# Placing a feed-forward part's ordinary units by a running count of VectorE work over TensorE work

## The chip, the cores and the metric

The kernel runs on one core of a Trainium2 chip. TensorE (PE in the profile) does the matmuls, VectorE (DVE) and ScalarE (ACT) the work on elements, GpSimd (POOL) a few small operations and some DMA issues, SyncE (SP) most DMA issues. Each engine takes its instructions in the order of the built program. The metric is the device time of one execution in microseconds; lower is better.

## The reference

Two decoder layers on 256 tokens of width 2048, all in float32:

```python
for l in range(DEPTH):                      # DEPTH = 2
    h = rms_norm(x, norm1_g[l])
    z = h @ w_in[l]                         # 2048 x 3584
    z_sgu = jax.nn.gelu(z[..., :2 * SGU_WIDTH], approximate=False)
    out_a = chunked_sgu(z_sgu, sgu_norm_g[l], sgu_w[l], sgu_b[l])
    out_b = swa_sink_attention(...)
    mixed = jnp.concatenate([rms_norm(out_a, out_norm_a[l]), rms_norm(out_b, out_norm_b[l])], axis=-1)
    x = x + mixed @ w_out[l]                # 2048 x 2048
    h2 = rms_norm(x, norm2_g[l])
    x = x + (jax.nn.silu(h2 @ w_gate[l]) * (h2 @ w_up[l])) @ w_down[l]   # 2048 x 5632, twice, and 5632 x 2048
```

The last line is the feed-forward part, and the only part that the change touches.

## The kernel before, in words

**Exact products.** PE multiplies in a reduced float32 form (`F32R`), so each operand is split into a high and a low part, and each product takes three matmuls (`mm3`, L126): high x high, high x low, low x high. The weights are split on the fly: a *unit* loads 256 x 512 weights into one of seven `raw` buffers (L88, queue of SP), ACT copies them into `wh` (L97), DVE subtracts into `wl` (L98); `wh` and `wl` have four buffers each.

**Two kinds of unit.** In the feed-forward part the 5632 columns are 11 blocks of 512. Blocks 3 to 10 are computed for gate and up together in a form like Strassen's, with seven products of half size in place of eight (`seven`, L571); I call their units *own units*. An own unit has 6 matmuls (`s_unit`, L574). A block has a *first half* (L588 to L607): four rounds of four own units, into four banks `m0` to `m3`. Three additions of weights on DVE stand before three of the four units of a round (L595, L598, L601), and one accumulating load by POOL (L603). At the *turn* the four banks are combined (L608 to L616). The *second half* (L619 to L628) has four rounds of three own units into banks `n0` to `n2`, without additions. Then the block is closed (L629 to L635), and its activations are transposed later (`act_later`, L567, due 2 and 3 ticks on; an ordinary unit is one tick, an own unit half of one).

Blocks 0 to 2, and all of the product with `w_down`, are *ordinary units* with 12 matmuls each (`unit`, L131), into one pair of banks `dacc` while the own units run. `gate_up` (L654) gives 16 units to a block; `down` (L668) gives units for one or two blocks at a time, for four column blocks in turn, and evacuates after each (L683). Before it may start, the activations of its blocks must have been transposed; until then it gives no unit, but says False (L670, L671): a *refusal*. `STD_ORDER` sets the order: gate and up of block 0, down of 0 and 3, gate and up of 1, down of 1 and 4, of 5 and 6, gate and up of 2, down of 2 and 7, of 8 and 9, of 10.

**How the two are mixed.** `s_stream` yields after every own unit and says by how much the ordinary stream, `other`, is owed (L696 to L703): 0.575 of a unit in a first half, 0.23 in a second half. When a whole unit is owed, one is emitted; at the turn and at the end of a block two are emitted whatever is owed. What is refused stays owed. When all own units are out, the rest of `other` runs alone (L705). A scheduler then orders each engine's instructions, with emission as priority, so that the built order follows the emitted one with small shifts.

Of the kernel before, what the change touches and what calls it, by code (L numbers as in the profile page):

```python
# [24 lines left out]
NTOK = SEQ // P  # L25
# [19 lines left out]
    ("gu", 0), ("down", (0, 3)), ("gu", 1), ("down", (1, 4)), ("down", (5, 6)), ("gu", 2),  # L45
    ("down", (2, 7)), ("down", (8, 9)), ("down", (10,)),
)
SHARE_A = 0.575
SHARE_B = 0.23
TURN = 2  # L50
RL = 512
WARM = 12

# [12 lines left out]
def trunk(ctx, tc, x, xt, w_in, w_out, w_gate, w_up, w_down, sgu_w, sgu_g, consts,  # L66
# [14 lines left out]
    def f(t):  # L81
        return t.bitcast(F32)
# [8 lines left out]
    def split2(raw):  # L91
        wh = wp.tile([P, 2, NB], F32R, tag="wh", name="wh", bufs=4)
        wl = wp.tile([P, 2, NB], F32R, tag="wl", name="wl", bufs=4)
        step = 2 if clock[0] > 1 else 1
        for j in range(0, 2, step):
            src = raw[:, j : j + step, :]
            nc.scalar.copy(wh[:, j : j + step, :], src)  # L97
            nc.vector.tensor_tensor(  # L98
                wl[:, j : j + step, :], src, f(wh[:, j : j + step, :]), ALU.subtract
            )  # L100
        return wh, wl

    clock = [0]
    serial = itertools.count()
    pending = []

# [24 lines left out]
    def unit(src, acts, acc, first, last):  # L131
        raw = raw_load(src, 2 if clock[0] < 4 else 1)
        wh, wl = split2(raw)
        for j in range(2):
            act, aj = acts[j]
            for t in range(NTOK):
                ts = slice(t * P, (t + 1) * P)
                mm3(
                    acc[t], act[:, 0, aj, ts], act[:, 1, aj, ts], wh[:, j, :], wl[:, j, :],
                    first and j == 0, last and j == 1,  # L140
                )
        tick()

    def product(srcs, pairs):
# [114 lines left out]
    for lay in range(L):  # L259
# [299 lines left out]
        def act_T(b, c, sg, pairs_f=pairs_f):  # L559
            ps = pm.tile([P, 2, SEQ], F32, tag="sm", name="ps_f")  # L560
            transpose_pair([sg[t][:, 2 * c * P : (2 * c + 2) * P] for t in range(NTOK)], ps)
            pair = tp.tile([P, 2, 2, SEQ], F32R, tag="aT", name="aT")
            nc.scalar.copy(pair[:, 0], ps)
            nc.vector.tensor_tensor(pair[:, 1], ps, f(pair[:, 0]), ALU.subtract)
            pairs_f.setdefault(b, []).append(pair)

        def act_later(b, sg, act_T=act_T):  # L567
            for c in range(2):
                later(2 + c, lambda c=c: act_T(b, c, sg))

        def seven(b, lay=lay, pairs2=pairs2, ext2=ext2, act_later=act_later):  # L571
            bank = [pa.tile([P, NB], F32, tag="acc", name=f"m{i}") for i in range(4)]

            def s_unit(raw, m, i, op, first, last):  # L574
                wh, wl = split2(raw)
                for j in range(2):
                    ah, al = (op(2 * i + j, h) for h in range(2))
                    mm3(bank[m], ah, al, wh[:, j, :], wl[:, j, :], first and j == 0, last and j == 1)
                tick(0.5)

            def a_op(k, t):
                return lambda p, h: pairs2[p][:, h, k, t * P : (t + 1) * P]

            def e_op(n):
                return lambda p, h: ext2[p][:, h, n, :]

            kept = []
            for i in range(4):  # L588
                b11 = raw_load(w_gate[lay, b, i, 0])
                b12 = raw_load(w_up[lay, b, i, 0])  # L590
                b22 = raw_load(w_up[lay, b, i, 1])
                t1 = wp.tile([P, 2, NB], F32, tag="raw", name="t1", bufs=7)
                t2 = ap.tile([P, 2, NB], F32, tag="spt", name="t2", bufs=4)
                first, last = i == 0, i == 3
                nc.vector.tensor_tensor(t1, b11, b12, ALU.add)  # L595
                s_unit(b11, 0, i, a_op(0, 0), first, last)
                yield SHARE_A
                nc.vector.tensor_tensor(t2, t1, b22, ALU.add)  # L598
                s_unit(t1, 1, i, e_op(1), first, last)
                yield SHARE_A  # L600
                nc.vector.tensor_tensor(b12, b12, b22, ALU.add)  # L601
                s_unit(t2, 3, i, e_op(2), first, last)
                nc.gpsimd.dma_start(t2, w_gate[lay, b, i, 1], accum_op=ALU.add)  # L603
                yield SHARE_A
                s_unit(b12, 2, i, e_op(0), first, last)
                yield SHARE_A
                kept.append(t2)  # L607
            m1 = zp.tile([P, NB], F32, tag="z", name="m1")  # L608
            nc.scalar.copy(m1, bank[0])
            u1 = zp.tile([P, NB], F32, tag="z", name="u1")  # L610
            nc.vector.tensor_tensor(u1, bank[3], m1, ALU.add)
            c22 = zp.tile([P, NB], F32, tag="z", name="c22")
            c21 = zp.tile([P, NB], F32, tag="z", name="c21")
            nc.vector.tensor_tensor(c21, bank[2], u1, ALU.add)
            nc.vector.tensor_tensor(c22, bank[1], c21, ALU.add)
            nc.vector.tensor_tensor(u1, bank[1], u1, ALU.add)  # L616
            yield "turn"
            bank = [pa.tile([P, NB], F32, tag="acc", name=f"n{i}") for i in range(3)]
            for i in range(4):  # L619
                b21 = raw_load(w_gate[lay, b, i, 1])  # L620
                b22 = raw_load(w_up[lay, b, i, 1])
                first, last = i == 0, i == 3
                s_unit(b21, 0, i, a_op(1, 0), first, last)
                yield SHARE_B
                s_unit(kept[i], 1, i, a_op(1, 1), first, last)
                yield SHARE_B
                s_unit(b22, 2, i, e_op(3), first, last)
                yield SHARE_B  # L628
            sg = [m1, c21]  # L629
            for t, m in ((0, m1), (1, c21)):  # L630
                nc.vector.tensor_tensor(m, bank[t], m, ALU.add)
                nc.scalar.activation(m, m, AF.Silu, scale=rstd2[t])
            nc.vector.tensor_tensor(u1, bank[2], u1, ALU.add)
            for t, c in ((0, u1), (1, c22)):
                nc.vector.scalar_tensor_tensor(sg[t], c, nrstd2[t], sg[t], ALU.mult, ALU.mult)  # L635
            act_later(b, sg)
            yield "turn"

        seven_done = [False]

# [13 lines left out]
        def gate_up(b, even=even, act_later=act_later):  # L654
            acc = yield from even(b, w_gate)
            sg = []
            for t in range(NTOK):
                s = zp.tile([P, NB], F32, tag="z", name="sg")
                nc.scalar.activation(s, acc[t], AF.Silu, scale=rstd2[t])
                sg.append(s)  # L660
            acc = yield from even(b, w_up)
            for t in range(NTOK):
                nc.vector.scalar_tensor_tensor(
                    sg[t], acc[t], rstd2[t], sg[t], ALU.mult, ALU.mult
                )
            act_later(b, sg)

        def down(blocks, final, lay=lay, pairs_f=pairs_f, norm_block=norm_block, ss1=ss1, pairs1=pairs1):  # L668
            for n in range(ND):
                while any(len(pairs_f.get(b, [])) < 2 for b in blocks):  # L670
                    yield False  # L671
                acc = new_acc() if seven_done[0] else new_acc(pd, "dacc")
                for k, b in enumerate(blocks):
                    for c in range(2):
                        pair = pairs_f[b][c]
                        unit(
                            w_down[lay, b, n, c], [(pair, 0), (pair, 1)], acc,
                            k == 0 and c == 0, k == len(blocks) - 1 and c == 1,
                        )
                        yield True  # L680
                for t in range(NTOK):
                    xs = xres[:, t, n * NB : (n + 1) * NB]
                    nc.vector.tensor_tensor(xs, acc[t], xs, ALU.add)  # L683
                    if final and lay == L - 1:
                        nc.sync.dma_start(out[t * P : (t + 1) * P, n * NB : (n + 1) * NB], xs)
                if final and lay < L - 1:
                    norm_block(n, ss1, pairs1, lay + 1, C_G1)
# [6 lines left out]
                    yield from down(what, k == len(STD_ORDER) - 1)  # L694

        other = std_stream()  # L696
        owed = 0.0
        for said in s_stream():
            turn = said == "turn"
            owed += TURN if turn else said  # L700
            for k in range(TURN):
                if (turn or (k == 0 and owed >= 1.0)) and next(other, False):
                    owed -= 1.0  # L703
        seven_done[0] = True
        for went in other:  # L705
            if not went:
# [89 lines left out]
```

## Time and profile before

| what | value |
|---|---|
| median of 3 runs | 2009.5 us (2006.13 to 2009.53) |
| the profiled execution, its own time | 2011.28 us |
| its span, first to last instruction | 2009.6 us |
| feed-forward part of layer 0, first own matmul of block 3 to the next layer's start | about 299 to 1004 us |
| the same of layer 1 | about 1300 to 2009 us |
| DMA, mean over the span | 226 GB/s, 453.80 MB |
| granted TensorE clock, mean | 0.995 |

How to read it: the span is what the hardware profiler saw of one execution. An engine's busy time is the union of its records. The records of matmuls overlap, since a matmul is issued while the one before it drains; how close PE is to its pace is seen from the distance of the starts, not from the busy share. "Idle before, releaser" tells which instruction ended an engine's wait. The granted clock is the share of TensorE's full clock that the throttle allowed.

### The profile page before, as it was taken

What the parts mean: (1) busy time and instruction counts of PE and PEld (TensorE: products, weight loads), DVE (VectorE), ACT (ScalarE), POOL (GpSimd) and SP (SyncE); (2) the same over time, 40 slices, a digit from 0 to 9 for tenths busy, and PEclk for the clock granted to TensorE, in tenths of its full rate; (3) what the DMA queues carried; (4) which work ended last, traced back from release to release, by engine and by line L of the source; (5) the groups of instructions that cost most, each with busy time, mean ns of one, the idle gap of its engine ahead of it and who ended that gap; (6) DMA issues with size and microseconds to landing.
All of it is one profiled execution on the core that took longest, in us unless ns stands there. A gap on an engine that the chain in (4) does not pass through costs nothing.

```text
span 2009.6 us, 24839 instructions
## 1 busy us (share of the span) xinstructions
PE 1971.9 (98%) x8942; PEld 1610.9 (80%) x8942; DVE 1664.0 (83%) x1931; ACT 1154.1 (57%) x1441; POOL 120.0 (6%) x129
## 2 busy tenths in 40 slices
PE   9999999999999999999999999999999999999999
PEld 6778887788878887788887788877888788877887
DVE  6767689989899897889866776889898998978896
ACT  6455566655655565555654655666556565555554
POOL 1211001000000000000002110000000000000000
PEclk9999999999999999999999999999999999999999
DMA  8753558787796876868655445487887878868684
GB/s 313 254 160 130 188 165 262 216 275 236 247 275 219 274 237 231 252 211 286 216 189 184 138 147 188 159 273 219 262 242 248 274 218 272 251 222 264 208 275 154
DMA packets 127772, 453.80 MB, mean 226 GB/s; under 512 B 14064, under 2 KB 16240, under 8 KB 127648
## 3 DMA queue, kind: packets, MB, share of 16 engines
q1 hardware_dynamic: 116288, 411.21, 60.1%
q0 software_dynamic: 11360, 41.00, 11.1%
q8 instruction: 70, 1.15, 0.2%
q14 instruction: 54, 0.44, 0.1%
HBM read 450.02 MB, written 4.23 MB: 226 GB/s over the span
## 4 chain that ended last, share of the span: by engine, by line
PE 83%; DVE 11%; issue 2%; DMA 2%; ACT 1%; POOL 1%; SPq 0%; DVEq 0%; POOLq 0%; ACTq 0%
PE dacc L128 11%; PE dacc L129 11%; PE dacc L127 10%; PE acc L128 8%; PE acc L129 8%; PE acc L127 7%; DVE wl L98 5%; PE m L129 4%; PE m L128 4%; PE m L127 4%; PE n L128 4%; PE n L129 4%; PE n L127 4%; DMA raw<-in_w_up_dram 1%; DVE raw L601 1%
## 5 line engine op out<-in xcount | busy, mean ns | idle before, releaser
L97 ACT CAST wh<-raw 128x1024 fp32r<-128x1024 f32 (+1 forms) x706 | 738.5, 1050 | 565.6 <-PE dacc L129 215.5
L98 DVE TENSOR_TENSOR wl<-raw,wh 128x1024 fp32r<-128x1024 f32 (+1 forms) x706 | 854.4, 1219 | 199.0 <-ACT wh L97 183.9
L97 ACT CAST wh<-t 128x1024 fp32r<-128x1024 f32 x192 | 202.3, 1054 | 186.9 <-PE dacc L129 109.7
L128 PE MATMUL dacc<-wl,aT 128*128 128x512 f32 x640 | 251.4, 393 | 8.5 <-DVE wl L98 8.5
L98 DVE TENSOR_TENSOR wl<-t,wh 128x1024 fp32r<-128x1024 f32 x192 | 233.5, 1222 | 21.5 <-ACT wh L97 16.3
L129 PE MATMUL dacc<-wh,aT 128*128 128x512 f32 x640 | 251.0, 392 | 0.0
L127 PE MATMUL dacc<-wh,aT 128*128 128x512 f32 x640 | 249.7, 392 | 0.7 <-DVE xres L683 0.7
L128 PE MATMUL acc<-wl,hT 128*128 128x512 f32 x448 | 177.0, 395 | 7.9 <-DVE wl L98 7.9
L127 PE MATMUL acc<-wh,hT 128*128 128x512 f32 x448 | 181.2, 407 | 0.8 <-ACT wh L97 0.8
L129 PE MATMUL acc<-wh,hT 128*128 128x512 f32 x448 | 177.1, 395 | 0.0
L127 PE MATMUL m<-wh,ext 128*128 128x512 f32 x384 | 153.3, 399 | 3.7 <-ACT wh L97 3.5
L128 PE MATMUL dacc<-wl,hT 128*128 128x512 f32 x384 | 150.5, 392 | 3.3 <-DVE wl L98 3.3
L128 PE MATMUL m<-wl,ext 128*128 128x512 f32 x384 | 150.6, 392 | 0.6 <-DVE wl L98 0.2
L127 PE MATMUL dacc<-wh,hT 128*128 128x512 f32 x384 | 150.7, 392 | 0.1
L129 PE MATMUL dacc<-wh,hT 128*128 128x512 f32 x384 | 150.2, 391 | 0.0
L129 PE MATMUL m<-wh,ext 128*128 128x512 f32 x384 | 150.0, 391 | 0.0
L128 PEld LDWEIGHTS dacc<-wl,aT 128*128 128x128 f32 x640 | 121.0, 189 | 36.1 <-DVE wl L98 11.1
L127 PEld LDWEIGHTS dacc<-wh,aT 128*128 128x128 f32 x640 | 120.8, 189 | 26.8 <-DVE xres L683 1.6
L129 PEld LDWEIGHTS dacc<-wh,aT 128*128 128x128 f32 x640 | 121.0, 189 | 25.0
L603 POOL DMA_DIRECT2D t<-in_w_gate_dram x64 | 54.5, 852 | 1387.2 <-DVE wl L98 754.6
L127 PE MATMUL acc<-wh,aT 128*128 128x512 f32 x320 | 126.9, 397 | 0.0
L129 PE MATMUL acc<-wh,aT 128*128 128x512 f32 x320 | 125.2, 391 | 0.0
(157 smaller groups left out, 3146.4 us busy)
## 6 DMA issues: line engine op xcount, KB each, us to landing
raw<-in_w_up_dram SPq DMA_DIRECT2D x240, 512.0 KB, 4.7
raw<-in_w_gate_dram SPq DMA_DIRECT2D x176, 512.0 KB, 4.7
raw<-in_w_down_dram SPq DMA_DIRECT2D x176, 512.0 KB, 4.6
raw<-in_w_in_dram SPq DMA_DIRECT2D x108, 512.0 KB, 4.3
raw<-in_w_out_dram SPq DMA_DIRECT2D x64, 512.0 KB, 3.3
t<-in_w_gate_dram POOLq DMA_DIRECT2D x64, 512.0 KB, 7.0
bias<-rdram POOLq DMA_DIRECT2D x8, 512.0 KB, 5.2
xr<-in_xt_dram SPq DMA_DIRECT2D x8, 256.0 KB, 5.7
```

What stands on the lines that cost most here:

```text
L97: nc.scalar.copy(wh[:, j : j + step, :], src)
L98: nc.vector.tensor_tensor(wl[:, j : j + step, :], src, f(wh[:, j : j + step, :]), ALU.subtract)
L127: nc.tensor.matmul(acc, ah, wh, start=first, stop=False)
L128: nc.tensor.matmul(acc, ah, wl, start=False, stop=False)
L129: nc.tensor.matmul(acc, al, wh, start=False, stop=last)
L601: nc.vector.tensor_tensor(b12, b12, b22, ALU.add)
L603: nc.gpsimd.dma_start(t2, w_gate[lay, b, i, 1], accum_op=ALU.add)
```

## The change

The fixed shares are gone. A running count, `debt`, grows by an estimate of every VectorE operation that is emitted in the feed-forward part (1.14 for a split or an addition of weights, 0.6 for an operation on a bank) and falls by 0.227 x 0.91 for every matmul, two for a group of transposes. After every own unit, and at the turn and the end of a block, ordinary units are emitted as long as the count is above zero and the stream does not refuse. The count is set to zero at the start of the part.

```diff
-SHARE_A = 0.575
-SHARE_B = 0.23
-TURN = 2
+VEC = 1.14
+VEC_P = 0.6
+MM = 0.227
+LOAD = 0.91
...
+        vec(1)
         return wh, wl
...
+    debt = [0.0]
+
+    def vec(n, cost=VEC):
+        debt[0] += n * cost
+
+    def pe(n):
+        debt[0] -= n * MM * LOAD
...
+        pe(12)
         tick()
...
             nc.vector.tensor_tensor(pair[:, 1], ps, f(pair[:, 0]), ALU.subtract)
+            vec(1, VEC_P)
+            pe(2)
...
                 nc.vector.tensor_tensor(t1, b11, b12, ALU.add)
                 s_unit(b11, 0, i, a_op(0, 0), first, last)
-                yield SHARE_A
+                vec(1)
+                yield
...
-            yield "turn"
+            vec(4, VEC_P)
+            yield
...
                 s_unit(b21, 0, i, a_op(1, 0), first, last)
-                yield SHARE_B
+                yield
...
+            vec(5, VEC_P)
             act_later(b, sg)
-            yield "turn"
+            yield
...
                     nc.vector.tensor_tensor(xs, acc[t], xs, ALU.add)
+                    vec(1, VEC_P)
...
         other = std_stream()
-        owed = 0.0
-        for said in s_stream():
-            turn = said == "turn"
-            owed += TURN if turn else said
-            for k in range(TURN):
-                if (turn or (k == 0 and owed >= 1.0)) and next(other, False):
-                    owed -= 1.0
+        debt[0] = 0.0
+        for _ in s_stream():
+            while debt[0] > 0.0 and next(other, False):
+                pass
         seven_done[0] = True
```

(`vec(1)` stands at the end of `split2`, `pe(12)` at the end of `unit`, and `pe(6)` at the end of `s_unit`. The second and third addition of a round are counted in the same way, and `gate_up` counts its two operations on banks with `vec(NTOK, VEC_P)`.)

More of the change, by code (lines that the diff above doesn't have):

```diff
@@ L578, in s_unit @@
                     mm3(bank[m], ah, al, wh[:, j, :], wl[:, j, :], first and j == 0, last and j == 1)
+                pe(6)
                 tick(0.5)
@@ L596, in seven @@
                 s_unit(b11, 0, i, a_op(0, 0), first, last)
-                yield SHARE_A
+                vec(1)
+                yield
                 nc.vector.tensor_tensor(t2, t1, b22, ALU.add)
                 s_unit(t1, 1, i, e_op(1), first, last)
-                yield SHARE_A
+                vec(1)
+                yield
                 nc.vector.tensor_tensor(b12, b12, b22, ALU.add)
@@ L603, in seven @@
                 nc.gpsimd.dma_start(t2, w_gate[lay, b, i, 1], accum_op=ALU.add)
-                yield SHARE_A
+                vec(1)
+                yield
                 s_unit(b12, 2, i, e_op(0), first, last)
-                yield SHARE_A
+                yield
                 kept.append(t2)
@@ L616, in seven @@
             nc.vector.tensor_tensor(u1, bank[1], u1, ALU.add)
-            yield "turn"
+            vec(4, VEC_P)
+            yield
             bank = [pa.tile([P, NB], F32, tag="acc", name=f"n{i}") for i in range(3)]
@@ L623, in seven @@
                 s_unit(b21, 0, i, a_op(1, 0), first, last)
-                yield SHARE_B
+                yield
                 s_unit(kept[i], 1, i, a_op(1, 1), first, last)
-                yield SHARE_B
+                yield
                 s_unit(b22, 2, i, e_op(3), first, last)
-                yield SHARE_B
+                yield
             sg = [m1, c21]
@@ L635, in seven @@
                 nc.vector.scalar_tensor_tensor(sg[t], c, nrstd2[t], sg[t], ALU.mult, ALU.mult)
+            vec(5, VEC_P)
             act_later(b, sg)
-            yield "turn"
+            yield
         seven_done = [False]
@@ L665, in gate_up @@
                 )
+            vec(NTOK, VEC_P)
             act_later(b, sg)
```

## The prediction

> **What bounds the kernel now.** I read first the busy row of the page, then how far the matmuls start apart, then the stretch of each block of the feed-forward part, then the chain of waits in a long block.
>
> ```profile
> PE 1971.9 (98%) x8942; PEld 1610.9 (80%) x8942; DVE 1664.0 (83%) x1931; ACT 1154.1 (57%) x1441; POOL 120.0 (6%) x129
> ```
>
> ```profile
> 386.32 0.40 PE L129 MATMUL m<-wh,ext 128*128 128x512 f32 x1
> 386.55 0.40 PE L127 MATMUL m<-wh,ext 128*128 128x512 f32 x1
> 386.79 0.39 PE L128 MATMUL m<-wl,ext 128*128 128x512 f32 x1
> ```
>
> PE is always "busy", but a record of 0.40 us begins every 0.23: the records overlap, so their sum tells little. The pace counts: 0.227 us a matmul, hence 1.36 us for an own unit (6 matmuls) and 2.72 for an ordinary unit (12). Seven blocks of layer 0 from first own matmul to the next block's (columns: stretch, its length, busy time of PE, PEld, DVE, ACT, POOL, granted clock, DMA share, GB/s):
>
> ```profile
> 298.90:381.20 82.30, 80.67 (x361) 66.26 (x360) 73.43 (x82) 53.67 (x62) 5.53 (x6) 1.00 0.76 237
> 381.20:468.10 86.90, 84.96 (x380) 69.10 (x378) 78.17 (x78) 49.81 (x52) 3.39 (x4) 1.00 0.78 242
> 468.10:550.90 82.80, 82.80 (x372) 68.35 (x370) 73.74 (x71) 50.04 (x52) 3.40 (x4) 1.00 0.82 255
> 550.90:637.50 86.60, 84.72 (x378) 69.06 (x377) 78.20 (x78) 49.58 (x52) 3.41 (x4) 1.00 0.78 242
> 637.50:720.10 82.60, 82.60 (x372) 68.42 (x370) 76.68 (x76) 49.02 (x50) 3.40 (x4) 1.00 0.80 255
> 720.10:806.80 86.70, 84.80 (x369) 69.24 (x368) 73.15 (x70) 50.04 (x52) 3.41 (x4) 0.98 0.77 243
> 806.80:897.40 90.60, 86.89 (x378) 69.92 (x377) 78.33 (x78) 49.67 (x52) 3.41 (x4) 0.98 0.76 232
> ```
>
> All but the first hold 28 own and 16 ordinary units: 28 x 1.36 + 16 x 2.72 = 81.7, and 8 transposes of 0.11: 82.6. Blocks 5 and 7 (468, 637) take just that: PE sets them alone. Blocks 4, 6 and 9 (381, 551, 807) have 8 more transposes (0.9) and lose 3.3, 3.0 and 7.0 us; block 8 (720) loses 4.1; the first, with 15 units, 2.4. With 0.7 for block 10 that is about 20 us a layer. In layer 1 the lengths repeat within 0.7, but block 8 takes 85.5. So **all that any placing can win is some 39 us** of 2009.6. In the long blocks the chain of waits turns from PE to DVE (381 to 404 us):
>
> ```profile
> by line: DVE wl L98 43.0%; DVE raw L601 14.8%; issue 11.7%; DVE t L598 10.3%; DVE t L595 9.9%; DVE aT L564 9.6%; DVE sg L663 5.7%; DVEq L598 0.1%
> ...
> 388.24 1.22 DVE L595 TENSOR_TENSOR t<-raw 128x1024 f32<-128x1024 f32 x1
> 389.37 1.22 DVE L98 TENSOR_TENSOR wl<-raw,wh 128x1024 fp32r<-128x1024 f32 x1
> 390.50 1.22 DVE L598 TENSOR_TENSOR t<-t,raw 128x1024 f32<-128x1024 f32 x1
> ```
>
> DVE paces at 1.136 us a split or addition. These are the places where the ordinary stream refuses (L671): `down` waits for activations that line 569 queues two and three ticks ahead. Six own units then pass alone, with too little PE work for their DVE work.
>
> **The change, part by part.** It adds no instruction to any queue: per engine the built programs hold the same counts, DMAs included. Only places move. A moved ordinary unit takes along its load on SP's queue (one of seven `raw` buffers), its copy on ACT (1.05 us; ACT is busy 50 of 83 us in a block), its split on DVE and its 12 matmuls. On SP it passes own units' loads; on POOL's queue only L603's accumulating loads stand here, one for four own units as before, and nothing passes them but with its own unit. I read the units off the recorded order. In layer 0, blocks 3 to 10 hold 15, 16, 16, 16, 16, 16, 16, 16 ordinary units before (127) and 13, 15, 14, 16, 16, 14, 15, 16 after (119); the second halves hold 4 or 5 before, and 1 to 3 after (7 in block 9). Eight move behind block 10, where 2.72 us of PE face 1.14 of DVE: same price there, 0.
>
> *Work sums.* An own unit of a first half costs DVE 1.136 and three of four another 1.136 for an addition; of a second half 1.136. A transpose group: DVE 0.6, PE 0.45. Line 663's pair: 1.32 (385.18 to 386.50). Closing a block (L631 to L635): 3 x 0.6 + 2 x 0.67 = 3.1. Now I sum from a block's first unit to the last refused one.
> Before, blocks 4 and 6: 8 own units, 6 additions, 1 ordinary: 15 x 1.136 + 1.8 + 1.32 + 3.1 = 23.3 on DVE; PE 8 x 1.36 + 2.72 + 1.35 = 15.0. DVE is short by 8.3, and the blocks lost 3.3 and 3.0: DVE came with a lead of about 5.1. Block 9, with 9 own units and 7 additions, is short by 9.2 and lost 7.0, of which 0.5 is its one bare group end and some 1.9 slow matmuls (below): lead 4.6. I take 5.0, which is what four `wl` buffers allow (3.7 own units).
> After, block 4: three ordinary units stand among the first six own. DVE 14 x 1.136 + 0.6 + 3.1 = 19.6 against 16.8, then six refused units: 10 x 1.136 + 1.32 + 1.2 = 13.9 against 9.1. Short by 7.6: loses 2.6.
> After, block 6: the refusal falls on the last six own units, behind 10 own and 6 ordinary: 31.6 against 30.9, then again 4.8. Short by 5.5: loses 0.5.
> After, block 9: it straddles the two halves, where an own unit needs no addition: DVE 2 own, 1 addition, 4 closings of L611 to L616 (2.4), 4 own of the second half, 1.32, 1.2: 12.9 against 9.1; before it 41.8 against 41.8. Short by 3.8, under the lead: 0 (up to 1.5, since L614 to L616 free the banks that these units write).
> So the refusals fall from 13.3 to 3.1: **-10.2 us a layer.**
>
> *Other block starts.* Blocks 5, 7, 8 and 10 now start with few ordinary units; by the same sums they are short by 3.8, 4.8, 4.8 and 5.5, where before the units at the turn covered them. With a lead of 5.0: +0.5; with 4.0: +3.2. I take **+1.5**.
>
> *Group ends in a run.* `dacc` has one pair of buffers. A group that begins straight after another waits for two evacuations:
>
> ```profile
> 862.18 1.28 DVE L683 TENSOR_TENSOR xres<-dacc,xres 128x512 f32<-128x512 f32 x2
> ...
> 862.92 0.50 PE L127 MATMUL dacc<-wh,aT 128*128 128x512 f32 x1 [0.38 <-DVE xres L683]
> ```
>
> The place costs 0.77 - 0.23 = 0.54 (862.15 to 862.92). Before has one a layer, after three: **+1.1** (0 if an own unit is moved between, 2.6 if each shows its whole 1.28).
> The Trainium skill speaks against the change here: "Perfetto Trace Analysis", Matmuls, says that independent groups should rotate through different PSUM banks, so that one's evacuation overlaps the next group's matmuls. By it the two new places show 2.6 in all, and the sum below would be 3 us smaller; the row showed less than half of an evacuation.
>
> *Block 8's 4.1 and 2.8.* ACT's copies came late there (it sat idle for 1.66 us before the one at 765.75, until PE gave a `wh` buffer free), at a turn with two ordinary units. After, the turn has two again. I count half as gone: **-1.7** (0 to -3.5).
>
> *The clock.* After a gap, matmuls run at 0.43 instead of 0.23 us:
>
> ```profile
> 826.28 0.39 PE L127 MATMUL m<-wh,ext 128*128 128x512 f32 x1
> 828.58 0.69 PE L128 MATMUL dacc<-wl,aT 128*128 128x512 f32 x1 [1.91 <-DVE wl L98]
> 829.07 0.63 PE L129 MATMUL dacc<-wh,aT 128*128 128x512 f32 x1
> 829.50 0.63 PE L128 MATMUL dacc<-wl,aT 128*128 128x512 f32 x1
> ```
>
> That is in block 9's 7.0 already, and goes with its gap.
> The Trainium skill ("TensorE: Matmul & The Clock Gate", Part 1) lets the clock drop after an idle window of about 3.4 us; here it dropped after 1.91 us idle, so the measurement decides; were the page right, the slow stretch would not hang on this gap, and 4 us of the sum would stay.
>
> *DMA.* First halves gain two loads on 28 x 0.5 MB in some 57 us. The densest stretch before, 897 to 950 us, moved 293 GB/s at a share of 0.93 with no PE gap. Cost 0.
>
> **Sum:** -10.2 + 1.5 + 1.1 - 1.7 = -9.3 a layer, at best -13 and at worst +7 (the lead, next part). The lead is fitted to three places of another order, so I take three quarters: -7 a layer, -14 in all. The profiled execution is 2011.28 us (span 2009.6 and 1.7 around it), the median 2009.5; the kernel's runs differ by 0.2%, so no change means within 4 us. 2009.5 - 14 = **1996**.
>
> **Rivals.**
> *The lead is thinner.* A second half gave DVE a lead from its four ordinary units, 4 x (2.72 - 1.14) = 6.3 us; now twelve bare own units give 12 x 0.22 = 2.7 and its closings take 2.4. If DVE comes to each block with 2 us instead of 5, blocks 4 to 10 lose 5.6, 1.8, 3.5, 2.8, 2.8, 1.8 and 3.5 = 21.8, and with 2.4 for block 3, 1.6 for group ends and 1.5 for the late copies 27: +7 a layer, **2024**. It decides from a lead under 3. For it: the built order breaks PE's groups of three matmuls, as it does where one waits for `wl`, at 68 places a layer against 58, ten of them in block 5 where none were. Against: `wl` has four buffers, and each second half still ends with an ordinary unit.
> *The gain is given back.* The refusals get cheaper, but late copies as in block 8 and stalls of 1 to 2 us at four block starts eat it: about -1 a layer, **2008**. For it: DVE's share of PE's time rises with eight ordinary units fewer per layer. Against: blocks 5 and 7 show that 0.89 (73.7 of 82.8) costs nothing.
> *It doesn't do what it says.* The scheduler could move units back; the recorded order shows second halves of twelve own units in a row, so this is out.
>
> **How the numbers follow.** Forecast 0.50, given back 0.24, thin lead 0.26. The first is faster but for 0.01; the second splits 0.07 faster, 0.12 same, 0.05 slower; the third 0.02 same, else slower. Faster 0.56, same 0.15, slower 0.29. Likeliest alone: 1983 to 2003 (twice -13, and half of the gain). To leave out no more than 0.2, the range reaches past "given back" and into the thin lead: 1983 to 2020.
>
> **What would show it.** Right: blocks 6 and 9 within 2 us of their matmul sum, block 4 within 3.5, no granted clock under 1.00 at block 9, the chain on PE there. Thin lead: DVE's splits in the chain at most block starts. Group ends: PE idle behind L683's like in blocks 4 to 6. Wrong altogether: blocks whose length grows in their second half, or DMA waits in first halves.

## The result, and the profile after

The changed kernel takes 1994.1 us (median of 4 runs, 1988.86 to 1997.43), the kernel before in the same session 2007.82 (4 runs, 2005.8 to 2009.53). The ratio is 0.9929, 95% interval 0.9916 to 0.9943: faster by 13.7 us. The profiled execution took 1988.86 us (span 1987.1), 22.4 less than the profiled execution of before. The profiles thus show more gain than the medians; more on that below.

The busy row of the changed kernel, with the same instruction counts as before:

```profile
PE 1961.3 (99%) x8942; PEld 1604.8 (81%) x8942; DVE 1659.2 (83%) x1931; ACT 1156.7 (58%) x1441; POOL 121.5 (6%) x129
```

PE's busy time fell by 10.6 us, less than half of the span's 22.5, with the same matmuls: the row doesn't tell where the time went. It has to be looked for in the stretches of the blocks. Blocks 3 to 9 of layer 0 in the changed kernel, each from its first own matmul to the next block's (stretch, length, busy time of PE, PEld, DVE, ACT, POOL, granted clock, DMA share, GB/s):

```profile
297.30:372.20 74.90, 74.90 (x337) 61.78 (x336) 69.06 (x78) 52.32 (x60) 5.81 (x6) 1.00 0.77 246
372.20:457.10 84.90, 81.55 (x363) 66.33 (x362) 73.72 (x73) 48.38 (x50) 3.38 (x4) 1.00 0.75 242
457.10:534.20 77.10, 77.10 (x345) 63.90 (x344) 71.33 (x70) 47.97 (x49) 3.40 (x4) 1.00 0.79 258
534.20:620.50 86.30, 85.35 (x382) 69.15 (x380) 78.64 (x78) 50.07 (x52) 3.40 (x4) 1.00 0.75 245
620.50:703.90 83.40, 83.13 (x371) 68.19 (x369) 76.46 (x76) 49.01 (x50) 3.41 (x4) 1.00 0.79 252
703.90:781.20 77.30, 77.00 (x342) 63.44 (x341) 70.22 (x68) 46.90 (x48) 3.40 (x4) 1.00 0.79 258
781.20:863.40 82.20, 82.09 (x372) 67.40 (x371) 77.73 (x77) 50.26 (x54) 3.41 (x4) 1.00 0.79 254
```

Where the length equals PE's busy time (297, 457), no gap is left. Blocks now hold 13 to 16 ordinary units, so lengths can't be set beside those of before; the loss can: length less matmuls at 0.227 us and transposes at 0.112.

| us lost in block | 3 | 4 | 5 | 6 | 7 | 8 | 9 | 10 | sum |
|---|---|---|---|---|---|---|---|---|---|
| before, layer 0 | 1.9 | 3.4 | 0.2 | 3.1 | 0 | 4.2 | 7.1 | 0.1 | 19.9 |
| after, layer 0 | 0.1 | 4.6 | 0 | 2.3 | 0.8 | 0.6 | 0.5 | 0 | 8.9 |
| before, layer 1 | 2.7 | 3.5 | 0 | 3.1 | 0 | 2.9 | 7.1 | 0.1 | 19.2 |
| after, layer 1 | 0.1 | 5.5 | -0.1 | 2.7 | 0.4 | 0.7 | 0.6 | 0.1 | 9.9 |

Together the blocks win 11.0 + 9.3 = 20.3 of the span's 22.5 us. Another 1.7 have nothing to do with the change: block 3 of layer 0 starts at 298.9 before and 297.3 after, because the profiled execution of before ran at a granted clock of 0.5 for 3.41 us at 129 us, ahead of all changed places. Block 9 is repaired: the row at 781 grants the clock 1.00 where before had 0.98. Block 4, where the forecast had a loss of 2.6, is worse than before. The chain of waits of the changed kernel there (384 to 414 us; share by line, then pieces with start and length):

```profile
by line: DVE wl L99 38.5%; DMA raw<-in_w_up_dram 23.1%; issue 15.8%; DVE raw L617 8.9%; DVE t L609 4.1%; DVE t L613 4.0%; DVE sg L682 3.9%; DVE aT L575 2.2%; PE m L138 1.7%; DVEq L613 0.1%
...
384.51 3.41 DVE wl L99 x3
...
401.81 6.94 DMA raw<-in_w_up_dram
```

It still runs through DVE's splits, as before (L99 and L617 are L98 and L601 of before, a few lines down), and now also through one load of `w_up` that is 6.94 us on its way. Taking the distances between the starts of PE's matmuls one by one, block 4 loses 2.2 us while units are refused (394 to 398 us), as forecast, and another 2.2 us at 411 us. DVE's timeline (start, length, instruction; in brackets the idle time before it and who ended it) shows what comes late there:

```profile
404.49 1.23 DVE L99 TENSOR_TENSOR wl<-raw,wh 128x1024 fp32r<-128x1024 f32 x1 [0.42 <-ACT wh L98]
406.34 1.23 DVE L609 TENSOR_TENSOR t<-raw 128x1024 f32<-128x1024 f32 x1 [0.63 <-DMA raw<-in_w_up_dram]
408.84 1.23 DVE L613 TENSOR_TENSOR t<-t,raw 128x1024 f32<-128x1024 f32 x1 [1.28 <-DMA raw<-in_w_up_dram]
```

and SP's queue (issues of loads, from the first issue to the end of the last, with their number at the end) what stood ahead of it:

```profile
385.67 11.33 SPq L89 DMA_DIRECT2D raw<-in_w_down_dram  x6
399.54 0.33 SPq L89 DMA_DIRECT2D raw<-in_w_gate_dram  x1
400.68 1.46 SPq L89 DMA_DIRECT2D raw<-in_w_up_dram  x2
404.09 9.74 SPq L89 DMA_DIRECT2D raw<-in_w_down_dram  x5
```

While `down` refuses, the count goes on growing; when the refusal ends, six ordinary units are emitted with hardly an own unit between, and their six loads of 512 KB go out ahead of the next own unit's. They are not issued at once: each waits on SP for a `raw` buffer that a split or an addition on DVE frees, so the six take 11.33 us, and the load of `w_up` that DVE waits for is issued 16.1 us after the first of them. DVE stands idle for additions that have no weights yet, and PE runs dry when the ordinary units are done. In layer 1 the same wait of DVE is 2.69 us and the loss 3.0. In the kernel before four loads of `w_down` stood there (394.02), and PE lost nothing behind them.

### The profile page after: what moved, and what is told of

Same layout as the page of the kernel before. It is cut to its first block, busy times and chain, and to the rows that moved or that the text cites. A ratio compares the mean times of both kernels' runs of the same rounds, so it can differ in the third digit from the quotient of the medians.

```text
span 1987.1 us, 24785 instructions
## 1 busy us (share of the span) xinstructions
PE 1961.3 (99%) x8942; PEld 1604.8 (81%) x8942; DVE 1659.2 (83%) x1931; ACT 1156.7 (58%) x1441; POOL 121.5 (6%) x129
## 3 DMA queue, kind: packets, MB, share of 16 engines
q8 instruction: 70, 1.15, 0.2%
## 4 chain that ended last, share of the span: by engine, by line
PE 80%; DVE 14%; issue 3%; DMA 2%; ACT 1%; POOL 1%; SPq 0%; DVEq 0%; POOLq 0%; ACTq 0%
PE acc L138 9%; PE acc L139 9%; PE acc L137 9%; PE dacc L138 9%; PE dacc L139 9%; PE dacc L137 9%; DVE wl L99 7%; PE m L138 4%; PE m L139 4%; PE m L137 4%; PE n L137 3%; PE n L139 3%; PE n L138 3%; DMA raw<-in_w_up_dram 2%; DVE t L613 1%
## 5 line engine op out<-in xcount | busy, mean ns | idle before, releaser
L98 ACT CAST wh<-raw 128x1024 fp32r<-128x1024 f32 (+1 forms) x706 | 739.4, 1051 | 585.0 <-PE dacc L139 214.5
L99 DVE TENSOR_TENSOR wl<-raw,wh 128x1024 fp32r<-128x1024 f32 (+1 forms) x706 | 852.3, 1218 | 191.0 <-ACT wh L98 181.8
L98 ACT CAST wh<-t 128x1024 fp32r<-128x1024 f32 x192 | 202.5, 1055 | 133.3 <-PE dacc L139 53.6
L99 DVE TENSOR_TENSOR wl<-t,wh 128x1024 fp32r<-128x1024 f32 x192 | 233.6, 1221 | 22.8 <-ACT wh L98 18.4
L138 PE MATMUL dacc<-wl,aT 128*128 128x512 f32 x576 | 225.6, 392 | 1.3 <-DVE wl L99 1.0
L139 PE MATMUL dacc<-wh,aT 128*128 128x512 f32 x576 | 224.5, 390 | 0.0
L137 PE MATMUL dacc<-wh,aT 128*128 128x512 f32 x576 | 223.6, 391 | 0.8 <-DVE xres L703 0.8
L137 PE MATMUL acc<-wh,aT 128*128 128x512 f32 x384 | 151.5, 395 | 0.0
L139 PE MATMUL acc<-wh,aT 128*128 128x512 f32 x384 | 149.9, 390 | 0.0
L138 PE MATMUL acc<-wl,aT 128*128 128x512 f32 x384 | 149.5, 389 | 0.0
L138 PEld LDWEIGHTS dacc<-wl,aT 128*128 128x128 f32 x576 | 108.1, 188 | 26.8 <-DVE wl L99 4.8
L137 PEld LDWEIGHTS dacc<-wh,aT 128*128 128x128 f32 x576 | 108.1, 188 | 24.8 <-issue 1.5
L139 PEld LDWEIGHTS dacc<-wh,aT 128*128 128x128 f32 x576 | 108.1, 188 | 22.4
```

The lines of the kernel that those rows point to most:

```text
L99: nc.vector.tensor_tensor(wl[:, j : j + step, :], src, f(wh[:, j : j + step, :]), ALU.subtract)
L137: nc.tensor.matmul(acc, ah, wh, start=first, stop=False)
L138: nc.tensor.matmul(acc, ah, wl, start=False, stop=False)
L139: nc.tensor.matmul(acc, al, wh, start=False, stop=last)
```

## Experiments

All times are medians of three rounds or more, beside the kernel before on the same chip at 2006.5 to 2008.6 us. Two explanations stood against each other at first. *Refusals*: what is lost is the own units that pass alone while `down` waits for its activations, and the change wins by standing more ordinary work among them. *Thin lead*: the running count leaves second halves bare, and DVE's lead at the next block is what decides.

**1 and 2. No refusals at all.** `STD_ORDER` gives block 1 and block 2 one place earlier, so that whenever `down` comes up its activations are long transposed. First in the kernel before, then in the changed one:

```diff
-    ("gu", 0), ("down", (0, 3)), ("gu", 1), ("down", (1, 4)), ("down", (5, 6)), ("gu", 2),
+    ("gu", 0), ("gu", 1), ("down", (0, 3)), ("down", (1, 4)), ("gu", 2), ("down", (5, 6)),
```

> The kernel before, with only the order of the ordinary stream changed (gate and up of block 1 directly behind that of block 0, that of block 2 ahead of down of 5 and 6), so that no ordinary unit is ever refused; the fixed rates stay. Refusal theory: blocks 4, 6 and 9 of each layer lose the 3.3, 3.0 and 7.0 us that they lose in the kernel before, so 26 us less, about 1982. Rival, that what pays is where the units lie (second halves bare, more in the first halves): the rates are as before, so less than 6 us, 2002 or more.

> The changed kernel with the same order of the ordinary stream, which leaves no refusal. Refusal theory: it saves what blocks 4, 6 and 9 still lose after the change (4.6, 2.4 and 0.5 us a layer, about 15 in all), and ends about 1979, level with the kernel before in that order. Rival, that the running count has a worth of its own beyond the refusals: it ends more than 6 us under the kernel before in that order.

Measured: the kernel before with this order 1975.51 us (ratio 0.9836, 0.9821 to 0.985), the changed one 1982.86 (0.9875, 0.986 to 0.989). Blocks 3 to 9 of the kernel before with the new order, same columns:

```profile
298.90:381.10 82.20, 80.57 (x360) 66.22 (x359) 73.30 (x81) 53.65 (x62) 5.52 (x6) 1.00 0.75 237
381.10:464.70 83.60, 83.60 (x380) 69.22 (x378) 74.91 (x73) 50.76 (x54) 3.39 (x4) 1.00 0.79 253
464.70:548.20 83.50, 83.50 (x378) 69.02 (x377) 77.80 (x78) 49.89 (x52) 3.41 (x4) 1.00 0.78 252
548.20:630.80 82.60, 82.60 (x372) 68.42 (x370) 76.66 (x76) 49.03 (x50) 3.41 (x4) 1.00 0.80 255
630.80:713.30 82.50, 82.50 (x370) 68.30 (x369) 73.37 (x70) 50.08 (x52) 3.40 (x4) 1.00 0.81 255
713.30:796.80 83.50, 83.50 (x378) 69.11 (x377) 77.94 (x78) 49.92 (x52) 3.41 (x4) 1.00 0.78 252
796.80:879.40 82.60, 82.60 (x372) 68.42 (x370) 76.69 (x76) 49.02 (x50) 3.40 (x4) 1.00 0.80 255
```

From block 4 on, length and PE's busy time agree to the hundredth: each such block holds 28 own and 16 ordinary units, as before, and takes just their matmuls. With refusals away, the fixed shares need no cure. 26 us were expected and 32 came, because block 8's late copies (4.1 and 2.8) went too. The running count, on the other hand, is 7 us *slower* than the fixed shares once nothing is refused, which neither of the two expectations of run 2 allowed for: blocks 4 to 9 lose 0.2 to 1.9 each, at starts and behind group ends. So with these constants the count is a cost where nothing is refused, and what it wins it wins around the refusals. Whether the cost comes from its bare second halves or from its bunching is not shown (run 8 was to tell).

**3. Bare second halves alone.** In the kernel before, with its refusals:

```diff
-SHARE_A = 0.575
-SHARE_B = 0.23
+SHARE_A = 0.72
+SHARE_B = 0.02
```

> The kernel before with other fixed rates, 0.72 in first halves and 0.02 in second halves, so that second halves are nearly bare as after the change; the refusals fall on the first units of blocks 4, 6 and 9 as before. Refusal theory: blocks 4, 6 and 9 keep their losses, within 3 us a layer of the kernel before, 2001 to 2013. Rival, that bare second halves and fuller first halves are what pays: about 1994.

Measured 2005.79 us (10 runs), ratio 0.9992 (0.9983 to 1.0002): no change. That is a sum of changes that cancel: in its profile, layer 0, block 4 lost 4.3 instead of 3.4 and block 6 6.7 instead of 3.1, block 9 less (4.4 instead of 7.1), and block 3's start and block 8's late copies were gone. So moving ordinary units from second into first halves is not the gain of the change. It does not clear the thin lead altogether: on the way into block 6's refusal DVE was never more than 1.6 us ahead in this run, and up to 4.1 in the kernel before (how this is measured is told further down), and that block lost more.

**4 and 6. One buffer fewer for `wh` and `wl`**, three in place of four, in the changed kernel and then in the kernel before:

```diff
-        wh = wp.tile([P, 2, NB], F32R, tag="wh", name="wh", bufs=4)
-        wl = wp.tile([P, 2, NB], F32R, tag="wl", name="wl", bufs=4)
+        wh = wp.tile([P, 2, NB], F32R, tag="wh", name="wh", bufs=3)
+        wl = wp.tile([P, 2, NB], F32R, tag="wl", name="wl", bufs=3)
```

> The changed kernel with three buffers instead of four for each of wh and wl. Buffer theory (the lead of VectorE over TensorE is what the buffers hold): the lead falls by an own unit, 1.4 us, and each of the six block starts and refusals that are near their lead loses that, some 8 to 12 us a layer, 2010 to 2018. Rival (the lead is set by how little VectorE has to spare, not by the buffers): under 4 us, up to 1998.

> The kernel before with three buffers for each of wh and wl. With three the changed kernel rose by 64 us. If that is what the missing buffer costs any placing, the kernel before rises by as much, to some 2071. If fuller second halves give VectorE a lead that bare ones do not (the thin lead), the kernel before rises by clearly less, 2045 or under, and is then faster than the changed kernel with three.

Measured 2058.71 us (ratio 1.0253, 1.0235 to 1.027) and 2067.61 (1.0285, 1.0265 to 1.0305). Run 4's size was missed by far; run 6 came near the 2071 that was expected if any placing pays the same. One buffer is worth 64 and 59 us. Nearly every half block loses something, second halves too, so the runs don't measure a lead at block starts alone. What they do say: the kernel before suffers as much as the changed one and stays behind it, so nothing here says that the changed order lives on a thinner reserve than the old one.

**5 and 11. Block 3's start.** Run 1 still lost 2.0 us there (the row at 298.90). The fixed share emits no ordinary unit among the first own units; the running count does after the first. Run 1 with half a unit owed from the beginning (5), and with that half taken back at the first turn (11):

```diff
-        owed = 0.0
+        owed = 0.5
+        first = True
...
+            if turn and first:
+                first = False
+                owed -= 0.5
```

(run 5 has the first two lines alone, without `first`)

> The kernel before in the order without refusals (as in the first experiment, 1975.5 us), and with half a unit owed from the start, so that the first ordinary unit stands behind the first own unit of block 3 as in the changed kernel. Block 3 lost 2.0 us a layer there and 0.2 in the changed kernel: 1975.5 - 3.6, about 1972. Rival, that half a unit owed moves all later units and brings back stalls at turns: 1976 or more.

> The kernel before in the order without refusals (1975.5), with half a unit owed from the start and taken back at the first turn, so that only block 3's first half is changed. Block 3 loses 2.0 us a layer without it, and lost 0.2 in the changed kernel and 0.9 and 0.4 with half a unit owed throughout: 1972 to 1974. If it is not under 1975, the start of block 3 is not to be had this way.

Measured 1978.74 us (0.9849, 0.983 to 0.9867) and 1975.76 (0.9836, 0.982 to 0.9852), against run 1's 1975.51. Run 5 missed: the half unit shifts every later emission, and blocks lost up to 1.1 where run 1 lost nothing. Run 11 cut block 3's loss to 0.7 and 0.8 in its profile, but its median is that of run 1: the gain of 2 us expected was not confirmed.

**7 and 9. Shorter refusals.** The activations of a block are queued at one due time instead of two:

```diff
-                later(2 + c, lambda c=c: act_T(b, c, sg))
+                later(2, lambda c=c: act_T(b, c, sg))
```

`down` then refuses for four own units instead of six. First in the changed kernel (7), then in the kernel before (9):

> The changed kernel with both groups of a block's transposes due after two ticks, where the second was due after three: refusals last four own units instead of six. Refusal theory: each of the two places with a loss (blocks 4 and 6: 4.6 and 2.4 us a layer) gives back up to two own units' shortfall, 2 x 0.8: some 3 us a layer, 1987 to 1990. Rival, that TensorE then waits for the activations to be transposed: no gain, 1994 or more.

> The kernel before with both groups of a block's transposes due after two ticks (the second was due after three): refusals last four own units instead of six; the fixed rates and the places of the refusals stay. In the changed kernel this edit took 2.4 and 2.0 us from blocks 4 and 6. Refusal theory: about 2 us from each of blocks 4, 6 and 9, and the slow matmuls of block 9, some 5 to 8 us a layer: 1993 to 1999, so that one number gives the kernel before most of what the running count gave. Rival, that the losses hang on the place of the refusal and not on its length: over 2003.

Measured 1980.0 us (0.9853, 0.9837 to 0.987) and 1985.97 (0.9884, 0.9869 to 0.9899): both gained more than expected. Blocks 4, 6, 8 and 9 of the kernel before with the short refusal:

```profile
383.40:467.60 84.20, 84.04 (x378) 69.11 (x377) 78.31 (x78) 49.30 (x52) 3.38 (x4) 1.00 0.78 252
...
550.10:633.90 83.80, 83.80 (x380) 69.20 (x378) 77.85 (x78) 49.41 (x52) 3.40 (x4) 1.00 0.77 251
...
716.40:801.80 85.40, 83.41 (x371) 68.21 (x369) 73.30 (x70) 50.14 (x52) 3.41 (x4) 1.00 0.77 247
801.80:887.20 85.40, 84.24 (x379) 69.02 (x377) 77.84 (x78) 49.29 (x52) 3.41 (x4) 1.00 0.79 246
```

Block 4 takes 84.2 in place of 86.9, block 6 83.8 in place of 86.6, block 9 85.4 in place of 90.6, and its clock is granted at 1.00. Block 8 (716) keeps its gap: 85.4 long, PE busy 83.4. So two own units fewer in the refusal, by an edit of one line, win 22 us: 8 more than the whole change. In the changed kernel the same line wins another 14 by the medians (8 by the profiles); block 4 falls from 4.6 to 2.1 and block 6 from 2.3 to 0.3 in layer 0, and the second half of block 9 loses 2.1, where it lost 0.4.

**8. The running count's distribution without refusals**, by fixed shares: run 1's order, `SHARE_A` 0.68 and `SHARE_B` 0.

> The kernel before in the order without refusals, with fixed rates of 0.68 in first halves and 0 in second halves: as many ordinary units within the own ones as in the changed kernel, and bare second halves, but evenly spaced. It tells why the running count, without refusals, came out 7 us over the fixed rates (1982.9 against 1975.5). If bare second halves and fewer ordinary units cost that, about 1983; if the count's bunching costs it, about 1976.

Measured 1987.3 us (0.9881, 0.9857 to 0.9906). It doesn't separate the two explanations, because of an accident in block 10 of layer 0, between two groups of `down`. PE's matmuls there in this run:

```profile
906.52 0.39 PE L129 MATMUL m<-wh,hT 128*128 128x512 f32 x1
909.09 0.47 PE L127 MATMUL dacc<-wh,aT 128*128 128x512 f32 x1 [2.18 <-DVE xres L683]
...
909.96 0.63 PE L127 MATMUL dacc<-wh,aT 128*128 128x512 f32 x1
910.38 0.63 PE L128 MATMUL dacc<-wl,aT 128*128 128x512 f32 x1
```

PE waits 2.18 us for the evacuation on DVE (L683), which stands in DVE's order behind a split and an addition and begins at 908.26, 2.7 us after the group's last matmul; and the matmuls behind it start 0.42 us apart instead of 0.227. Block 10 loses 5.7 us by it; blocks 3 to 9 lose some 4 in sum.

**10. Block 8's late copies.** In the kernel before, one ordinary unit instead of two at block 8's turn:

```diff
-            yield "turn"
+            yield "turn" if b != 8 else "one"
...
-            turn = said == "turn"
+            turn = said in ("turn", "one")
...
-            for k in range(TURN):
+            for k in range(1 if said == "one" else TURN):
```

> The kernel before with one ordinary unit instead of two at the turn of block 8 alone; all else keeps its place but for one unit that comes later in that block's second half. If the late copies at that turn (4.1 and 2.8 us) hang on the two ordinary units queued there behind the evacuation of a gate product, they go: 2007.5 - 7, about 2001. If not, within 3 us of the kernel before.

Measured 2003.46 us (10 runs; 0.9975, 0.9965 to 0.9985), 4.8 of the 7 us expected; block 8's loss fell from 4.1 and 2.8 to 1.4 in each layer. The place in the kernel before, ACT's timeline (start, length, instruction, in brackets the idle time before it and who ended it):

```profile
767.11 1.05 ACT L97 CAST wh<-raw 128x1024 fp32r<-128x1024 f32 x1 [0.31 <-PE m L129]
769.58 1.04 ACT L97 CAST wh<-t 128x1024 fp32r<-128x1024 f32 x1 [1.42 <-PE n L129]
770.53 1.26 ACT L659 ACTIVATE sg<-dacc,ir 128x512 f32<-128x512 f32 x2
```

The copy at 769.58 is for a later own unit. It waits for PE to free a `wh` buffer, the two ordinary units queued at the turn hold such buffers, and behind it in ACT's order the evacuation of `dacc` (L659) and further copies wait too. With one unit fewer queued, half of the copies' 2.8 us is gone in both layers. The other 1.3 of layer 0's 4.1 are matmuls that start 0.43 us apart between 772 and 774 us, a stretch at half clock that neither layer 1 nor run 10 has there.

**12. The burst behind the refusal.** The changed kernel, with at most two ordinary units after an own unit:

```diff
-            while debt[0] > 0.0 and next(other, False):
-                pass
+            for _ in range(2):
+                if debt[0] <= 0.0 or not next(other, False):
+                    break
```

> The changed kernel, with at most two ordinary units emitted after an own unit in place of as many as the count asks for. In block 4 the refusal is followed by two ordinary units, an own unit, two more, and so on, where the changed kernel emits six ordinary units between two own ones. The refused units themselves keep their place. In the changed kernel's profile block 4 loses 2.2 us while units are refused (PE idle at 394 and 397 us) and 2.2 more, 3.0 in layer 1, at 411 us, where VectorE waited for a load of w_up that stood behind six loads of w_down and took 6.94 us. If the burst is what makes that load late, block 4 loses 2.0 to 3.0 in both layers, the refused part stays at 2.2, and the span is 1981 to 1984 us (1987.1 before); the median falls by 3 to 6 us from 1994. If the load is late for another reason (the refusal itself, or the general load on the DMA engines), block 4 still loses over 4 us and span and median stay within 2 us of the changed kernel's.

Measured 1988.95 us (5 runs, 1986.28 to 1991.83; ratio 0.991, 0.9896 to 0.9923), 5 under the changed kernel's median, as expected of the burst. SP's queue in this run now mixes the loads:

```profile
388.68 1.46 SPq L89 DMA_DIRECT2D raw<-in_w_down_dram  x2
393.40 0.33 SPq L89 DMA_DIRECT2D raw<-in_w_gate_dram  x1
395.68 2.60 SPq L89 DMA_DIRECT2D raw<-in_w_up_dram  x2
402.55 11.04 SPq L89 DMA_DIRECT2D raw<-in_w_down_dram  x8
```

Block 4 loses 2.7 and 3.2 in place of 4.6 and 5.5: of the stall behind the late load nothing is left in layer 0 and 0.45 us in layer 1, and the 2.2 of the refused units stay. The burst is what made the load late: behind two loads of `w_down` in place of six, the same load of `w_up` is issued 9.3 us after the first of them (16.1 before) and is 4.8 us on its way (6.94 before). A burst need not cost that much, though. Run 7 issues six loads of `w_down` in a row too, DVE waits 1.43 us for `w_up` behind them, and PE loses 0.3 us there. The span, however, was expected at 1981 to 1984 and is 1989.2 in this run's profile, since the shifted units cost more elsewhere (block 6 3.0 and 3.6, block 7 1.6 and 2.5). So the place is settled; its worth for the whole kernel is not, since the intervals of the two ratios still overlap a little (0.9916 to 0.9943 without the limit).

**The best version** is the kernel before with run 1's order: 1975.51 us, 18.6 less than the changed kernel's median (1994.1), with one line of the order moved. Run 11 equals it.

## Why the prediction was right, and where its steps were not

The forecast was 1996 us, and 1994.1 came. The mechanism held: the gain comes from the refusals above all, and runs 1, 7 and 9 show that shortening or removing them wins 14 to 32 us, while run 3, which moves units between halves only, wins nothing. The rivals fell: the time is neither 2024 nor 2008, and DVE does not come to the blocks with a thinner lead than before. In block 6's first own unit, the time from the end of the split to the matmul that reads it is 1.66 us in the changed kernel and 1.84 in the kernel before. The terms, per layer (layer 0 / layer 1, from the table and the distances of matmul starts; block 9's own group end of before is left inside the refusals, as in the forecast's 7.0):

| term | forecast | measured |
|---|---|---|
| refused units, blocks 4, 6, 9 | -10.2 | -10.1 / -9.6 |
| starts of blocks 5, 7, 8, 10 | +1.5 | +1.2 / +1.1 |
| group ends in a run | +1.1 | +0.6 / +0.6 |
| block 8's late copies | -1.7 | -4.1 / -2.8 |
| DMA | 0 | +2.2 / +3.0 |
| block 3's start | not in the sum | -1.9 / -2.6 |
| small rest | | +1.1 / +1.0 |
| sum | -9.3 | -11.0 / -9.3 |

**Refusals.** Blocks 4, 6 and 9 were to lose 2.6, 0.5 and 0 while units are refused; they lost 2.2, 1.2 and 0.1 (layer 1: 2.2, 1.8, 0.1). The slow clock of block 9 went with its gap, as forecast, though such a gap does not bring it every time (last section). The lead behind this can be measured: pair each split on DVE with the first matmul that reads its buffer, and take the time between. PE's timeline, with the matmul that reads a split which DVE ended at 385.65, and the longest wait among the refused units:

```profile
385.73 0.47 PE L138 MATMUL dacc<-wl,hT 128*128 128x512 f32 x1
...
397.83 0.50 PE L137 MATMUL m<-wh,ext 128*128 128x512 f32 x1 [1.21 <-ACT wh L98]
```

The lead there is 0.1 us. It was 3.0, 2.6 and 1.7 at the three own units in a row just before, which spent it, and an ordinary unit brought it back to 1.3 at the last own unit ahead of the refusal. In block 6 it was 3.1 at that point, and the loss is 1 us smaller. In the kernel before, block 4 went in with 3.7. So the lead is no stock of 5.0 that each block start finds: in block 4 of the kernel before it runs from 3.7 down to 0.1. The fitted 5.0 gave nearly the right sum all the same, probably because the work ahead of the refusal was counted along with it; that is argued, not shown. A quarter was taken off the sum for doubt in this number, and the terms built on it came out right.

**DMA is the step that failed** inside a forecast that came true. It was costed at 0 from a stretch of before with a high rate and no gap. That looked at rates, not at the order in SP's queue. The bursts of loads that come with a burst of ordinary units were in the recorded order; what they stand ahead of was not asked. Run 12 takes the burst away, and of the stall of 2.2 and 3.0 us nothing and 0.45 are left. A wait for DMA in a first half was the sign named for a wrong forecast; it came at this one place a layer.

**Late copies**: half was counted as gone, all of it went, and with it layer 0's 1.3 us of slow matmuls. Run 10 shows what they hang on in the kernel before: the second ordinary unit queued at the turn. That the changed kernel has two units at that turn too was no ground for halving.

**Block 3's start** was in the ceiling (2.4) and not in the sum. The running count emits an ordinary unit after the first own one, and the loss falls to 0.1. Runs 5 and 11 agree in their profiles, less clearly in their times.

**Block starts** came as counted, at other places: 0.8 and 0.6 in blocks 7 and 8, none in blocks 5 and 10.

**Group ends**: three were counted in each layer of the changed kernel, and one shows, in block 6. At every other place matmuls of own units stand between two groups, the case for which the forecast had named 0. PE's timeline:

```profile
586.57 0.39 PE L139 MATMUL dacc<-wh,aT 128*128 128x512 f32 x1
587.34 0.47 PE L137 MATMUL dacc<-wh,aT 128*128 128x512 f32 x1 [0.38 <-DVE xres L703]
```

0.77 from start to start, 0.54 over the pace: the price named. The Trainium skill ("Perfetto Trace Analysis", Matmuls) wants independent groups in different PSUM banks, so that an evacuation is hidden. In the changed kernel 0.54 of the two evacuations' 1.28 us showed, at that one place a layer; in run 8's block 10, behind 906.52, 2.34 us did, more than the whole. So a whole evacuation as the price was too high where DVE was on time, and too low where it was late.

**The shading** from -9.3 to -7 a layer is what brought the forecast to the median. By the profiles (22.4 us) the unshaded sum, -18.6, was the nearer one. So the nearness of 1996 to 1994.1 is in part luck. The profiled execution of before, 2011.28 us, was slower than all four of its comparison runs, and the profiled one of the changed kernel was the fastest of its four (the others 1993.84, 1994.36, 1997.43); the loss table sets these two side by side. Where the others spent 5 to 8 us more was not profiled, but the granted clock that is on record for each points to slow stretches: spans of 1987.1, 1992.1, 1992.7 and 1995.7 us go with mean clocks of 0.998, 0.997, 0.995 and 0.994. In the same way the profile of before has six stretches at half clock and that of the changed kernel two (and one in its last microsecond); at up to 1.7 us each (half of 3.41) that is an estimated 6 to 7 of the 22.4 us, of which block 9's two went with their gaps. And the sum is right with errors that cancel: DMA against late copies and block 3.

## What to carry to other kernels

Before tuning how fill-in work is spread, look for the places where it is not to be had at all: removing the dependency that made the filler refuse won 32 us, more than twice what a better placing around the refusal won, and the better placing then cost 7. A balance that goes on counting while the filler is refused pays out in a burst, and the burst's loads stand in the queue ahead of what the next unit needs: follow the queue's order, not its mean rate. A lead of one engine over another is not a stock either: measure it at the place, as the time between a producer's end and its first use.

## What the runs showed of the hardware

After some gaps of PE, matmuls start 0.42 to 0.43 us apart, nearly half pace: after 1.91 us in block 9 of the kernel before and after 2.18 us in run 8. The Trainium skill ("TensorE: Matmul & The Clock Gate", Part 1) puts the drop behind an idle window of about 3.4 us. Both gaps here were shorter, so by these runs less idle time is enough.

The length of the gap alone does not decide. A gap of 1.89 us in run 10 (layer 1, 1822.12 us) was followed by full pace, and so was the longest of the changed kernel, in block 4 of layer 1:

```profile
1400.56 0.39 PE L137 MATMUL m<-wh,hT 128*128 128x512 f32 x1
1403.55 0.50 PE L138 MATMUL m<-wl,hT 128*128 128x512 f32 x1 [2.60 <-DVE wl L99]
1403.89 0.40 PE L139 MATMUL m<-wh,hT 128*128 128x512 f32 x1
```

Two short gaps of 0.76 and 1.13 us in block 8 of the kernel before, on the other hand, did bring slow matmuls. What decides shows in the granted clock that the traces record. The stretches at half clock that end inside the span last 3.41 us (in runs 4 and 6 some are two in a row), and within one trace they start whole multiples of 3.413 us apart: in the kernel before at 770.70, 828.73, 1088.14, 1129.10 and 1828.83 us, 17, 76, 12 and 205 steps. Lay a grid of such steps over a trace and add up PE's idle time in each step of the feed-forward parts. In the 14 traces every step with 1.87 us idle or more is followed by a stretch at half clock, and none with 1.85 or less is. The 1.91 us of block 9 and the two gaps of block 8 (1.90 together) fell into one step each; the 2.60 us of the changed kernel were cut into 1.45 and 1.15. Where the grid lies differs from execution to execution, so the same gap costs up to 1.7 us more in one execution than in another. An estimate from the record: a stretch lowers the mean clock of a span of 2000 us by 0.00085, hence 2 us of time for 0.001 of mean clock; of the 41 executions of the kernel before that stand beside the experiments, the six with a mean of 0.998 have spans of 2003.1 to 2005.0 us, and the five with 0.993 or 0.994 have 2009.2 to 2011.8.

The fourth `wh`/`wl` pair was worth 59 to 64 us (runs 4 and 6), more than all that any placing could win (39 us).
